# Odd attention: the second output projection begun inside the last block

## The chip, the cores and the metric

The kernel runs on one core of one Trainium2 chip. The metric is the time on the device, in microseconds, of one execution. Before the change it is 1584.4 us, the median of three runs (1583.5 to 1587.77).

## The reference

Two transformer layers work on `x` (512 tokens, width 1024) with a context of 256 tokens. Layer 0 is "even" (a gated MLP over chunks, and differential attention), layer 1 is "odd" (attention over a sliding window, with the context and a learned sink). Each layer ends with a SwiGLU network, and a last norm closes the block. The change lies in the odd layer and in the start of its SwiGLU:

```
def sink_attend(q, kvs, sink):                 # 16 heads, 4 KV heads, so 4 heads in a group
    ...                                        # scores of a block of 128 queries: window of up to 384 keys, masked, and 256 context keys
    p = softmax(concatenate(scores + [s_sink]))
    ...                                        # out = sum over the parts of p @ v

y = o.reshape(b, s_len, C_Q_WIDTH) @ w_out     # odd_mixer, 1024 x 1024
...
h = h + g1 * y
h = h + g2 * swiglu(modulate(h, norm2_g[l], sh2, sc2), ffn_w_in[l], ffn_w_out[l])
...
return rmsnorm(h, final_g)                     # modulate is rmsnorm(x, g) * (1 + scale) + shift
```

## The kernel before

Activations lie transposed in SBUF: 8 tiles of 128 features by 512 tokens. Every float32 product is made of three matmuls of rounded parts (`mm3`, lines L107, L108, L109): high weight by high input, high weight by low input, low weight by high input. So each input and each weight has a high and a low part. A weight block is loaded by SP's DMA queue into a "raw" tile (L78); ScalarE casts it to the high part (L81); the low part is a subtraction (L84), on GpSimd (POOL), or on VectorE where `dve_lo` says so (with 1, all of them). These tiles come from a ring of raw tiles and weight slots, `open_ring(width, raw, bufs)`; in the odd layer it has 3 raw tiles and 4 slots. `split` does the same for inputs: a cast on ScalarE (L123) and a subtraction on VectorE or POOL (L124).

`odd` projects keys, values and queries, and then computes attention. `attend(g, half)` handles one group of four heads for one half of the queries, in two blocks of 128 queries. For each head of a block `softmax` issues the scores (L1384, L1389, L1392), VectorE's maximum (L1395) and ScalarE's exponential (L1398). The exponentials are transposed on TensorE (L1421), copied out of PSUM by ScalarE or VectorE in turn (L1424), and multiplied with the values (L1432). Per group and half, a transposed row of reciprocals (L1439, L1443) scales the outcome (L1445).

All four groups run for the first half of the queries; `keep` splits their eight output tiles into `cat`. Then all four run for the second half. On TensorE the first half's output projection, `project(0, ...)`, is there to fill the gaps of the second half's attention: it takes the `fill` bank of PSUM (names `pf` in the profile). Then come, in the order of the program:

- `ffn_rstd`: the mean square of the first half's new residual (L157, L162), its inverse root on VectorE (L166 to L140), a diagonal of it (L177), and the product that spreads this over the partitions as a row (L187), into the same fill bank. This is "root's row" below.
- `catB`: eight `keep` of the second half, low parts in turn on VectorE and POOL.
- `ffn_open`, which starts the transfers of the SwiGLU's first weights (`ffn_in`, L817), their casts (L948) and subtractions (L952).
- `ffn_mod`: the modulation of the first half (L856 on VectorE, L857 on ScalarE, then L123 and L124).
- `project(1, ...)`: eight blocks of 8 x 3 matmuls of 256 columns, each followed by the residual (L778) and the square (L791, L795).

The SwiGLU's first products with the first half (the "direct" ones, of `ax` tiles) come next, then the second half's root, its row and its modulation, and the products with the second half (tiles `T` and others).

The order on each engine isn't that of the program. A scheduling layer moves instructions by a timeline of its own, within what the tile pools and banks allow; `issue_after` keeps what it encloses behind a given instruction. On each engine instructions then run in the order so fixed.

Of the kernel before, what the change touches and what calls it, by code (L numbers as in the profile page):

```python
# [15 lines left out]
D = 1024  # L16
KT = D // P
TX = 512
TC = 256
# [7 lines left out]
class Builder:  # L27
# [1275 lines left out]
    def odd(self):  # L1303
        tc, nc, a = self.tc, self.nc, self.a
        self.wp.release()
        self.open_wide()
        self.open_ring(512, 3, 4)
        X, C = [[[t[:, c] for t in A] for A in self.A] for c in (slice(0, TX), slice(TX, TA))]
        self.hcp.release()
        Rk = tc.alloc_tile_pool(name="kv1", bufs=1, side="right", reuse_waits="tile")  # L1310
# [13 lines left out]
        K = []  # L1324
# [31 lines left out]
        Qs = {}  # L1356

        def project_q(n):
            ps = self.fill()
# [5 lines left out]
        def softmax(g, i, rc):  # L1365
# [9 lines left out]
            for x in range(4):  # L1375
                pair, par = x // 2, x % 2
                if edge:
                    two = self.wide() if par == 0 else two
                    ps = two[:, par * TX:par * TX + TX]
                else:  # L1380
                    ps = self.wide()
                Q = Qs[2 * g + pair][par][:, i * P:(i + 1) * P]
                for p in range(2):
                    nc.tensor.matmul(ps[:, st:en], Q, K[g][p][:, b0 * P:b1 * P], start=p == 0, stop=p == 1,  # L1384
                                     skip_group_check=True)
                for b in range(b0, b1):
                    if b != i:
                        m0, c = (b - i + 1) * P, st + (b - b0) * P
                        nc.tensor.matmul(ps[:, c:c + P], identr, mask[:, m0:m0 + P], start=False, stop=True,  # L1389
                                         skip_group_check=True)  # L1390
                for p in range(2):
                    nc.tensor.matmul(ps[:, en:en + TC], Q, K[g][p][:, TX:], start=p == 0 and not edge, stop=p == 1,  # L1392
                                     skip_group_check=True)
                c = nm[:, x:x + 1]
                nc.vector.tensor_reduce(c, ps[:, st:en + TC], axis=AX, op=ALU.max, negate=True)  # L1395
                nc.vector.tensor_tensor(c, c, nsink[:, 4 * g + x:4 * g + x + 1], ALU.min)
                e = Rs.tile([P, 640], F32, name=self.uid("e"), tag="e1", bufs=7)
                nc.scalar.activation(e[:, :w + TC], ps[:, st:en + TC], AF.Exp, bias=c, accum_out=sums[:, x:x + 1])  # L1398
                es.append(e)
# [47 lines left out]
        raw = {}  # L1447

        def keep(half, n, eng):
            t = self.axp.tile([P, TA], F32R, name=self.uid("ax"), tag="ax", bufs=16)  # L1450
            t = t[:, :TC], t[:, TC:TX]
            self.split(*t, raw[half, n // 2][:, n % 2, :], eng)
            return t

        cat = []
# [7 lines left out]
            attend(g, 1)  # L1463
        sq = self.sumsq()

        def project(half, cat, bank):
            for m in range(KT):
                ps = bank(m)[:, :TC]
                self.dense(ps, self.blocks(a["odd_out"][m]), cat)
                self.residual(1, 2, m, half * TC, TC, ps)  # L1470
                self.square(sq, m, half * TC, TC, rest[half], (8, 7)[half])

        rest = [], []
        project(0, cat, lambda m: self.fill())
# [105 lines left out]
```

## Time and profile before

| | us |
|---|---|
| median of three runs | 1584.4 |
| the profiled execution | 1584.4 |
| its span | 1582.6 |
| TensorE busy (PE) | 1520.8 (96%) |
| VectorE busy (DVE) | 1080.4 (68%) |
| GpSimd busy (POOL) | 825.5 (52%) |
| ScalarE busy (ACT) | 725.9 (46%) |

The mean granted TensorE clock is 0.991. The odd layer's attention ends at about 1188 us, the projection of the second half follows up to about 1220, with the first SwiGLU products among its matmuls, and the SwiGLU of this layer takes the rest but for the last norm. TensorE's matmuls overlap, so the time from one start to the next, not an instruction's own duration, is its cost. In a row of the timeline the figure in square brackets is idle time of the engine just before, with what ended it. Buffer numbers are left out in the profile; in the changed program the attention's lines behind the scores have a number higher by one (L1421 is L1422, and so on).

### The profile page before, as it was taken

How to read it: one execution, taken by the hardware profiler on the slowest of the kernel's cores; microseconds unless marked ns; L12 is line 12 of the kernel's file. 1: busy time of each engine (PE TensorE's matmuls, PEld its weight loads, DVE VectorE, ACT ScalarE, POOL GpSimd, SP SyncE). 2: the span in 40 equal slices, each digit the busy share in tenths (PEclk: the TensorE clock that was granted, in tenths of full speed). 3: DMA queues.
4: the chain of work that ended last, by engine and by line, in shares of the span. 5: the costliest groups of instructions: out<-in, count | busy, mean ns of one | idle time of the engine just before them, and what ended most of it. 6: DMA issues, size and time to landing. Idle time of an engine off the chain costs nothing.

```text
span 1582.6 us, 25033 instructions
## 1 busy us (share of the span) xinstructions
PE 1520.8 (96%) x9575; PEld 1356.2 (86%) x9575; DVE 1080.4 (68%) x1951; ACT 725.9 (46%) x1477; POOL 825.5 (52%) x556
## 2 busy tenths in 40 slices
PE   6999988999999999999999989999999999999998
PEld 4676877889999999999999978777869989999997
DVE  3620788775697787888786495666568976666665
ACT  2422677553553333333333244556556544444444
POOL 0464211060347776777776415541304299898982
PEclk9999999999999999999999989999999999999999
DMA  9735100033123333454552012110225233333301
GB/s 329 309 128 202 44 8 1 1 133 134 67 74 120 113 109 118 139 160 143 165 167 67 27 52 80 61 34 8 68 76 197 65 112 106 99 105 107 98 21 54
DMA packets 53415, 162.26 MB, mean 103 GB/s; under 512 B 6192, under 2 KB 8624, under 8 KB 45616
## 3 DMA queue, kind: packets, MB, share of 16 engines
q1 hardware_dynamic: 46240, 135.37, 25.1%
q10 hardware_dynamic: 7056, 25.30, 4.9%
q8 instruction: 75, 1.23, 0.3%
q14 instruction: 44, 0.36, 0.1%
HBM read 158.55 MB, written 2.10 MB: 102 GB/s over the span
## 4 chain that ended last, share of the span: by engine, by line
PE 85%; DVE 9%; ACT 4%; issue 2%; DMA 0%; SPq 0%; POOL 0%; DVEq 0%; ACTq 0%; POOLq 0%
PE pw L107 11%; PE pw L108 11%; PE pw L109 11%; PE pb L108 8%; PE pb L109 8%; PE pb L107 8%; PE pf L107 4%; PE pf L108 4%; PE pf L109 4%; PE pb L1432 2%; PE pb L1421 2%; PE pf L363 2%; PE pw L1384 1%; PE pw L1392 1%; DVE t L883 1%
## 5 line engine op out<-in xcount | busy, mean ns | idle before, releaser
L84 POOL TENSOR_TENSOR w<-raw,w 128x512 fp32r<-128x512 f32 (+1 forms) x84 | 127.4, 1523 | 243.7 <-ACT w L81 221.7
L108 PE MATMUL pw<-ax,w 128*128 128x384 f32 (+2 forms) x732 | 234.6, 321 | 3.8 <-DVE ax L470 2.5
L107 PE MATMUL pw<-ax,w 128*128 128x384 f32 (+2 forms) x732 | 233.5, 323 | 4.1 <-DVE q L883 1.9
L109 PE MATMUL pw<-ax,w 128*128 128x384 f32 (+2 forms) x732 | 233.8, 320 | 0.1
L778 DVE SCALAR_TENSOR_TENSOR xT<-pb,mod,xT 128x512 f32<-128x512 f32 (+3 forms) x208 | 145.9, 707 | 125.8 <-PE pb L109 125.5
L883 POOL TENSOR_TENSOR w<-raw,w 128x512 fp32r<-128x512 f32 x110 | 169.0, 1551 | 19.7 <-ACT w L883 19.5
L883 POOL TENSOR_TENSOR w<-t,w 128x512 fp32r<-128x512 f32 x99 | 149.7, 1515 | 55.6 <-ACT w L883 55.6
L107 PE MATMUL pb<-hh,w 128*128 128x512 f32 x480 | 171.0, 356 | 1.2 <-DVE xT L778 1.2
L109 PE MATMUL pb<-hh,w 128*128 128x512 f32 x480 | 171.6, 357 | 0.3 <-DVE w L883 0.3
L108 PE MATMUL pb<-hh,w 128*128 128x512 f32 x480 | 171.2, 357 | 0.0
L108 PE MATMUL pw<-T,w 128*128 128x384 f32 (+1 forms) x508 | 157.1, 310 | 1.2 <-DVE T L124 1.2
L107 PE MATMUL pw<-T,w 128*128 128x384 f32 (+1 forms) x508 | 156.3, 310 | 1.1 <-DVE hs L883 1.1
L109 PE MATMUL pw<-T,w 128*128 128x384 f32 (+1 forms) x508 | 157.1, 310 | 0.0
L107 PEld LDWEIGHTS pw<-ax,w 128*128 128x128 f32 x732 | 138.9, 190 | 12.4 <-DVE q L883 2.6
L108 PEld LDWEIGHTS pw<-ax,w 128*128 128x128 f32 x732 | 139.3, 190 | 11.7 <-DVE ax L470 3.4
L107 PE MATMUL pf<-ax,w 128*128 128x256 f32 (+2 forms) x420 | 140.1, 333 | 8.5 <-DVE qf L256 5.7
L109 PEld LDWEIGHTS pw<-ax,w 128*128 128x128 f32 x732 | 139.5, 191 | 3.1 <-DVE w L952 0.4
L108 PE MATMUL pf<-ax,w 128*128 128x256 f32 (+2 forms) x420 | 138.9, 331 | 0.0
L109 PE MATMUL pf<-ax,w 128*128 128x256 f32 (+2 forms) x420 | 138.7, 330 | 0.0
L883 POOL TENSOR_TENSOR hh<-hs,hh 128x768 fp32r<-128x768 f32 (+1 forms) x42 | 80.2, 1910 | 90.0 <-ACT hh L883 67.6
L883 POOL TENSOR_TENSOR w<-rawo,w 128x512 fp32r<-128x512 f32 x59 | 103.7, 1758 | 28.7 <-ACT w L883 28.7
L232 DVE SCALAR_TENSOR_TENSOR junk<-ar,cb 128x1024 bf16<-128x1024 f32 x64 | 105.6, 1651 | 0.0
(376 smaller groups left out, 3937.1 us busy)
## 6 DMA issues: line engine op xcount, KB each, us to landing
raw<-ffn_in SPq DMA_DIRECT2D x44, 1024.0 KB, 5.2
ar<-ada SPq DMA_DIRECT2D x24, 1024.0 KB, 6.7
ar<-ada ACTq DMA_DIRECT2D x48, 512.0 KB, 3.6
rawo<-ffn_out SPq DMA_DIRECT2D x88, 256.0 KB, 3.0
raw<-odd_out SPq DMA_DIRECT2D x32, 256.0 KB, 2.7
raw<-qk SPq DMA_DIRECT2D x16, 256.0 KB, 8.2
raw<-uv SPq DMA_DIRECT2D x16, 256.0 KB, 2.7
raw<-even_out SPq DMA_DIRECT2D x8, 512.0 KB, 3.5
```

Of the source, the lines that this page charges most:

```text
L84: eng.tensor_tensor(lo, raw, hi.bitcast(F32), ALU.subtract)
L107: mm(out, s[0], m[0], start=start, stop=False, **kw)
L108: mm(out, s[0], m[1], start=False, stop=False, **kw)
L109: return mm(out, s[1], m[0], start=False, stop=stop, **kw)
L232: return self.nc.vector.scalar_tensor_tensor(junk, t, 1.0, self.cb[who], ALU.mult, ALU.mult, accum_out=self.acc[who][:, col:col + 1])
L363: nc.tensor.matmul(ps[32 * q:32 * q + 32, :w], cst[:, k, :], t[:, w * q:w * q + w], start=k == 0, stop=k == KT - 1, skip_group_check=True)
L778: ins = self.nc.vector.scalar_tensor_tensor(h, ps[:, r], self.modcol(l, j, m, who), h, ALU.mult, ALU.add)
L883: tail[key] = fn(*args, **kw)
L1384: nc.tensor.matmul(ps[:, st:en], Q, K[g][p][:, b0 * P:b1 * P], start=p == 0, stop=p == 1, skip_group_check=True)
L1392: nc.tensor.matmul(ps[:, en:en + TC], Q, K[g][p][:, TX:], start=p == 0 and not edge, stop=p == 1, skip_group_check=True)
L1421: last = nc.tensor.transpose(pt[:, x * P:(x + 1) * P], es[2 * (x % 2) + x // 2][:, kb * P:(kb + 1) * P], self.ident)
L1432: nc.tensor.matmul(po[64 * h:64 * h + 64, :], V[vb][:, 64 * g:64 * g + 64], t[:, h * TC:h * TC + TC], start=kb == 0, stop=kb == nb - 1, sk ...
```

## The change

Five things change in `odd`.

1. The ring gets 4 raw tiles and 5 slots instead of 3 and 4, for the whole layer.
2. `project(1)` begins early. For its blocks m = 0 and 1, the products with the first three groups' tiles (k = 0 to 5, 36 matmuls of 256 columns) go into the two halves of one fill bank, block m behind the last score matmul of head x = 1 (m = 0) or 2 (m = 1) in the last block of the last group. The products with the last group (k = 6, 7) and the residual follow when that group is done.
3. `catB` splits its first six tiles on VectorE alone (three of them were POOL's); the last two stay as they were.
4. `dve_lo` is set to 1 after the first early block instead of before `project(1)`.
5. Root's row is made behind all this, in a bank of `wide` instead of the fill bank; `ffn_mod` may issue only behind the split of the last group's first tile.

```diff
-        self.open_ring(512, 3, 4)
+        self.open_ring(512, 4, 5)
...
-                    nc.tensor.matmul(ps[:, en:en + TC], Q, K[g][p][:, TX:], start=p == 0 and not edge, stop=p == 1,
-                                     skip_group_check=True)
+                    last = nc.tensor.matmul(ps[:, en:en + TC], Q, K[g][p][:, TX:], start=p == 0 and not edge,
+                                            stop=p == 1, skip_group_check=True)
+                scored[g, i, x] = last
...
-            self.split(*t, raw[half, n // 2][:, n % 2, :], eng)
+            self.kept[n] = self.split(*t, raw[half, n // 2][:, n % 2, :], eng)
...
-        def project(half, cat, bank):
-            for m in range(KT):
+        def project(half, cat, bank, ready=()):
+            for m, ps, W in ready:
+                for k in (6, 7):
+                    self.mm3(ps, W[k], cat[k], False, k == 7)
+                self.residual(1, 2, m, half * TC, TC, ps)
+                self.square(sq, m, half * TC, TC, rest[half], (8, 7)[half])
+            for m in range(len(ready), KT):
...
-        self.ffn_rstd(sq, rest[0], TX // 2)
-        catB = [keep(1, n, nc.gpsimd if n % 2 else nc.vector) for n in range(8)]
+        dg = self.rstd_diag([(sq[:, :TC], TC)], 1.0 / D, self.fill, None, None, rest[0])[0]
+        catB = [keep(1, n, nc.vector) for n in range(6)]
+        both, ready, mark = self.fill(), [], None
+        for m in range(2):
+            W = self.blocks(a["odd_out"][m])
+            ps = both[:, m * TC:(m + 1) * TC]
+            with tc.issue_after(scored[(3, *((3, 1), (3, 2))[m])].ins):
+                for k in range(6):
+                    with tc.issue_after(mark.ins) if mark else ExitStack():
+                        ins = self.mm3(ps, W[k], catB[k], m == k == 0, False)
+            mark = ins
+            ready.append((m, ps, W))
+            if m == 0:
+                self.dve_lo = 1
+        catB += [keep(1, n, nc.gpsimd if n % 2 else nc.vector) for n in range(6, 8)]
+        self.r = self.spread(dg, self.wide)
         Rs.release()
         Rk.release()
         self.ffn_open(1)
-        self.ffn_mod(1, 0)
-        self.dve_lo = 1
-        project(1, catB, lambda m: self.bank())
+        with tc.issue_after(self.kept[6].ins):
+            self.ffn_mod(1, 0)
+        project(1, catB, lambda m: self.bank(), ready)
```

On TensorE, in the last block of the last group, these instructions stood between the last scores (`pw_11235` with `qb_10320`) and the first product with the last head's transposed weights (`pt_11264`). `e_11252` is the exponential of those last scores.

```order
L1392 MATMUL pw_11235<-kh_9187,qb_10320 128x256
L1392 MATMUL pw_11235<-kl_9188,qb_10320 128x256
L1421 MATMUL pb_11259<-ident_100,e_11243 128x128
L1421 MATMUL pb_11259<-ident_100,e_11233 128x128
L1421 MATMUL pb_11266<-ident_100,e_11243 128x128
L1421 MATMUL pb_11266<-ident_100,e_11233 128x128
L1421 MATMUL pb_11259<-ident_100,e_11252 128x128
L1421 MATMUL pb_11266<-ident_100,e_11252 128x128
L1432 MATMUL pb_11258<-pt_11264,v_2_9364 64x256 x2
```

Now 29 of the early matmuls stand ahead of those scores. Behind the scores, after two transposes and one more early matmul, TensorE has this up to the first transpose of `e_11252`; `pf_11653` is the fill bank, and L187 is root's row.

```order
L107 MATMUL pf_11653<-ax_11647,w_11689 128x256
L1433 MATMUL pb_11166<-pt_11204,v_5_9370 64x256 x2
L1422 MATMUL pb_11266<-ident_100,e_11224 128x128
L1422 MATMUL pb_11266<-ident_100,e_11243 128x128
L1422 MATMUL pb_11266<-ident_100,e_11233 128x128
L108 MATMUL pf_11653<-ax_11647,w_11689 128x256
L109 MATMUL pf_11653<-ax_11647,w_11689 128x256
L107 MATMUL pf_11653<-ax_11650,w_11689 128x256
L108 MATMUL pf_11653<-ax_11650,w_11689 128x256
L109 MATMUL pf_11653<-ax_11650,w_11689 128x256
L187 MATMUL pw_11716<-q_11632,ones 128x256
L1422 MATMUL pb_11259<-ident_100,e_11252 128x128
```

Seven early matmuls, root's row, one more transpose (L1422) and the two products L1433 have come in between.

On VectorE, at the end of the attention, the last group's scaling (L1445) stood behind the eight L856 of the modulation. What is shown begins with the last two of these.

```order
L856 SCALAR_TENSOR_TENSOR hh_11671<-xT_636_3306,mod_69,pf_11635 128x256
L856 SCALAR_TENSOR_TENSOR hh_11670<-xT_636_3306,mod_69,pf_11635 128x256
L1445 TENSOR_TENSOR o_11113<-o_11113,pb_11296 128x512
L84 TENSOR_TENSOR w_11797<-raw_11795,w_11797 128x512
L124 TENSOR_TENSOR ax_11655<-o_11113,ax_11655 128x256
```

Now the scaling and the first split come first, then the L856, whose last two are shown with what follows:

```order
L856 SCALAR_TENSOR_TENSOR hh_11728<-xT_636_3306,mod_69,pw_11716 128x256
L856 SCALAR_TENSOR_TENSOR hh_11727<-xT_636_3306,mod_69,pw_11716 128x256
L84 TENSOR_TENSOR w_11840<-raw_11838,w_11840 128x512
L124 TENSOR_TENSOR ax_11737<-hm_11734,ax_11737 128x256
L778 SCALAR_TENSOR_TENSOR xT_633_3300<-pf_11653,mod_69,xT_633_3300 128x256
L84 TENSOR_TENSOR w_11874<-raw_11872,w_11874 128x512
L778 SCALAR_TENSOR_TENSOR xT_634_3302<-pb_11793,mod_69,xT_634_3302 128x256
```

The L856 have moved behind L1446 (L1445 before) and the split of the last group's first tile.

On ScalarE, the casts of the first `ffn_in` weights (L948) stood early in the second projection, between casts of its weights (`w_11802`, `w_11836`):

```order
L81 CAST w_11802<-raw_11800 128x512
L948 CAST w_12038<-raw_11666 128x512
L948 CAST w_12041<-raw_11666 128x512
L948 CAST w_12044<-raw_11666 128x512
L948 CAST w_12047<-raw_11666 128x512
L81 CAST w_11836<-raw_11834 128x512
```

Now they stand behind the casts of all its weights and behind the squares (L791) of all residuals but the last:

```order
L81 CAST w_11996<-raw_11994 128x512
L791 ACTIVATE q_11907<-xT_635_3304 128x256
L791 ACTIVATE q_11946<-xT_635_3304 128x256
L791 ACTIVATE q_11985<-xT_636_3306 128x256
L948 CAST w_12037<-raw_11723 128x512
L948 CAST w_12040<-raw_11723 128x512
```

The first of them waits until the projection's seventh block (m = 6) has released the slot that the tile takes; POOL's subtractions L952 follow them.

More of the change, by code (lines that the diff above doesn't have):

```diff
@@ L1355, in odd @@
         Rs = tc.alloc_tile_pool(name="att1", bufs=1, side="right", reuse_waits="tile")
-        Qs = {}
+        Qs, scored = {}, {}
         def project_q(n):
@@ L1445, in attend @@
             nc.vector.tensor_tensor(o, o, ps, ALU.mult)
-        raw = {}
+        raw, self.kept = {}, {}
         def keep(half, n, eng):
```

## The prediction

> **What bounds the kernel now.** I first read the page: the share of each engine and the chain of work that ended last.
>
> ```profile
> PE 1520.8 (96%) x9575; PEld 1356.2 (86%) x9575; DVE 1080.4 (68%) x1951; ACT 725.9 (46%) x1477; POOL 825.5 (52%) x556
> PE 85%; DVE 9%; ACT 4%; issue 2%; DMA 0%; SPq 0%; POOL 0%; DVEq 0%; ACTq 0%; POOLq 0%
> ```
>
> TensorE is busy for 1520.8 of 1582.6 us and makes up 85% of the chain. The change neither adds a product nor takes one away: the 36 matmuls that it starts early are among the 192 that followed the attention. So it can only win or lose time in which TensorE stands still, or runs at a lower clock. I looked for that time with the busy table in 10 us stretches around the end of the attention (columns: length, PE, PEld, DVE, ACT, POOL, granted clock, DMA share, GB/s).
>
> ```profile
> 1180.00:1190.00 10.00, 7.90 (x49) 4.76 (x48) 5.36 (x15) 3.91 (x10) 0.61 (x1) 0.83 0.56 211
> 1190.00:1200.00 10.00, 8.36 (x63) 7.53 (x63) 8.96 (x13) 10.00 (x26) 7.09 (x7) 1.00 0.39 131
> 1270.00:1280.00 10.00, 8.10 (x58) 7.26 (x57) 9.90 (x14) 4.74 (x10) 9.93 (x7) 1.00 0.48 158
> ```
>
> TensorE loses 2.1 us in 1180-1190, where the clock also falls to 0.83, and 1.6 us in 1190-1200. In 1270-1280 it loses 1.9 us, and there VectorE is the full engine (9.90). The list of TensorE's waits in 1150-1290 names five of the losses (us in total, times, longest); its timeline shows the others, in brackets, and what follows them.
>
> ```profile
> PE pw L107 <- DVE q L883: 1.9, 1, 1.9
> PE pb L109 <- DVE w L84: 1.6, 1, 1.6
> PE pw L107 <- DVE hs L883: 1.1, 1, 1.1
> PE pf L187 <- DVE sa L1400: 1.1, 1, 1.1
> PE pb L109 <- DVE w L883: 0.3, 1, 0.3
> ```
>
> ```profile
> 1165.62 0.65 PE L1432 MATMUL pb<-pt,v 128*64 128x256 f32 x4
> 1166.20 0.66 PE L1421 MATMUL pb<-ident,e 128*128 128x128 f32 x4
> ...
> 1182.07 0.44 PE L1421 MATMUL pb<-ident,e 128*128 128x128 f32 x2 [1.48 <-ACT e L1398]
> 1183.13 0.65 PE L1432 MATMUL pb<-pt,v 128*64 128x256 f32 x4 [0.62 <-ACT pt L1424]
> 1183.72 0.74 PE L1421 MATMUL pb<-ident,e 128*128 128x128 f32 x4
> 1184.39 1.12 PE L1432 MATMUL pb<-pt,v 128*64 128x256 f32 x4
> 1185.44 1.11 PE L1421 MATMUL pb<-ident,e 128*128 128x128 f32 x4
> 1186.48 1.60 PE L1432 MATMUL pb<-pt,v 128*64 128x256 f32 x8
> 1188.01 0.66 PE L1443 MATMUL pb<-ident,pt 128*128 128x128 f32 x4
> 1188.63 0.28 PE L108 MATMUL pb<-ax,w 128*128 128x256 f32 x1
> ...
> 1189.93 0.28 PE L107 MATMUL pb<-ax,w 128*128 128x256 f32 x1
> ```
>
> The last block of the last group of heads has no other matmuls left to issue. TensorE stands 1.48 us while the exponential of the last scores runs, then 0.62 us for a copy of the transposed weights. Right after, the same instructions take nearly twice as long: four L1432 take 1.05 us from start to start (1184.39 to 1185.44) against 0.58 at 1165.62, and four L1421 are busy for 1.11 us against 0.66. Two stretches of 2 us show why; the seventh column is the granted clock.
>
> ```profile
> 1184.00:1186.00 2.00, 2.00 (x11) 0.99 (x10) 0.00 (x0) 0.58 (x1) 0.07 (x1) 0.54 1.02 426
> 1186.00:1188.00 2.00, 2.00 (x11) 0.74 (x9) 1.41 (x4) 0.00 (x0) 0.00 (x0) 0.61 0.98 410
> ```
>
> **Part by part.** The rows are those of the profiled execution, which took 1584.4 us (span 1582.6, 1.8 around it). That is also the median of the three runs, so the sum needs no shift.
>
> *The fill in the last block.* A projection matmul on 256 columns starts every 0.118 us (1188.63 to 1189.93, 11 steps). The 36 early ones are 4.3 us, moved from behind the attention into its last block, in themselves worth nothing. 29 of them stand ahead of the last scores and only delay these. The other 7 (0.8 us) stand between the last scores and the first transpose that needs the exponential, along with L1433 x2 (0.3), one more transpose (0.15) and root's row (0.5) that did not stand there. That makes 1.8 us for a wait of 1.48 us. The exponential comes a little later itself, because ScalarE now has a cast of 0.6 us of an output weight ahead of it; I allow 0.2 us. 1.8 covers 1.7, barely: **-1.5** (bounds 0 and -1.5). The 0.62 us wait on the copy has the same work around it as before, and stays.
>
> *The clock.* Against full speed the slow steps lose 0.47 (L1432 x4), 0.45 (L1421 x4) and 1.53 - 1.16 = 0.37 us (L1432 x8), together **-1.3** if the clock stays up (bounds 0 and -1.4). It fell after 2.1 us of standing in 2.5 us. The waits of 1.6 and 1.9 us in the list lie in 1190-1200 and 1270-1280, whose clock is 1.00. With 0.6 to 0.7 us left here I expect no drop.
>
> [...]
>
> *Root's row and the modulation.* The row (L187) leaves this place:
>
> ```profile
> 1163.99 0.67 PE L187 MATMUL pf<-q,ones 128*128 128x256 f32 x2 [1.09 <-DVE sa L1400]
> 1164.50 0.38 PE L1421 MATMUL pb<-ident,e 128*128 128x128 f32 x2
> 1163.55 0.69 ACT L1398 ACTIVATE e<-pw,sa 128x512 f32<-128x512 f32 x1 [2.31 <-DVE sa L1396]
> ```
>
> The transposes behind it can't start before their exponential ends at 1164.24, so its 0.51 us gives back only 0.26 here, and costs 0.51 in the last block: **+0.3** (bounds 0 and +0.5). VectorE's eight L856 (3.2 us), which stood ahead of the last block's own output (L1445), now stand behind it and the first subtraction of catB; nobody on the path waits for them until the first ffn_in product. Three subtractions of catB pass from POOL to VectorE, some 0.4 us each (the L795 below has their shape), while VectorE is half idle (5.36 in 1180-1190). SP's first transfers of ffn_in now queue behind an output weight whose slot comes free in the last block, some 4 us later than before; they land in 5.2 us and are first read over 20 us on, so that costs nothing.
>
> ```profile
> raw<-ffn_in SPq DMA_DIRECT2D x44, 1024.0 KB, 5.2
> ```
>
> *The projection after the attention.* These rows carry it (VectorE and POOL):
>
> ```profile
> 1197.29 1.66 DVE L84 TENSOR_TENSOR w<-raw,w 128x512 fp32r<-128x512 f32 x1
> 1198.88 1.78 DVE L952 TENSOR_TENSOR w<-raw,w 128x512 fp32r<-128x512 f32 x1
> 1207.15 0.68 DVE L84 TENSOR_TENSOR w<-raw,w 128x512 fp32r<-128x512 f32 x1
> 1207.75 0.41 DVE L795 TENSOR_TENSOR sq<-sq,q 128x256 f32<-128x256 f32 x1
> 1209.87 0.48 DVE L778 SCALAR_TENSOR_TENSOR xT<-pb,mod,xT 128x256 f32<-128x256 f32 x1
> 1197.14 9.80 POOL L952 TENSOR_TENSOR w<-raw,w 128x512 fp32r<-128x512 f32 x6
> ```
>
> A weight's subtraction on VectorE takes 0.68 us alone and 1.66 to 1.78 us while POOL subtracts too, and the late one stops TensorE for the 1.6 us of the list. In the changed order POOL's L952 come only after the sixth block of the projection, and the weights of the first 46 matmuls behind the attention have been subtracted within it. But VectorE's queue gets tight. From its L1446 to the residual of the seventh block stand 9 L84 (6.1 us), 8 L856 (3.2), 7 L778 (3.4), 5 L124 (2.1), 4 L795 (1.6) and L1446 (0.7): 17.1 us, less some 0.08 us overlap for each of 34 (1207.15 + 0.68 against 1207.75), so 14.4. POOL's five L124 will slow one or two of them by 1 us: about 16 us, against 134 matmuls or 15.8 us of TensorE. I expect half the wait to come back in small pieces: **-0.8** (bounds 0 and -1.6; the first rival has it above zero).
>
> *VectorE's lead into the FFN.* 45 matmuls now lie between the second root's row and the first product with the second half, 30 before; so VectorE's modulation starts 15 x 0.118 = 1.8 us earlier against TensorE.
>
> ```profile
> 1229.88 0.87 DVE L856 SCALAR_TENSOR_TENSOR hm<-xT,mod,pb 128x256 f32<-128x256 f32 x2 [1.72 <-PE pb L187]
> 1252.65 0.41 DVE L989 TENSOR_TENSOR hs<-hs,pw 128x256 f32<-128x256 f32 x1
> ```
>
> From 1229.88 VectorE works without a gap to 1252.65, and TensorE then waits for it 0.3 + 1.1 + 1.9 = 3.3 us over the next 25 us (the list's L883). What starts 1.8 us earlier should end so, unless ScalarE or POOL step in: **-1.2** (bounds 0 and -1.8).
>
> *The larger ring* takes effect at the start of the layer:
>
> ```profile
> 955.11 0.62 ACT L81 CAST w<-raw 128x512 fp32r<-128x512 f32 x1 [3.07 <-issue]
> 957.42 0.39 PE L108 MATMUL pw<-ax,w 128*128 128x256 f32 x1 [0.72 <-DVE ax L205]
> 984.73 0.47 PE L107 MATMUL pf<-ax,w 128*128 128x512 f32 x1 [2.62 <-DVE qf L256]
> ```
>
> ScalarE stood 3.07 us on a cast whose slot was taken, behind which the normalised inputs queue that TensorE waits 0.72 us for. A fifth slot frees the cast: **-0.7**. POOL's order shifts as well, by one or two subtractions of 1.3 us ahead of the rotated keys on which the 2.62 us wait rests: bounds -0.7 and +1.0.
>
> Sum: -1.5 - 1.3 + 0.3 - 0.8 - 1.2 - 0.7 = -5.2; 1584.4 - 5.2 = **1579.2 us**. All terms at their good ends: -1.5 - 1.4 - 1.6 - 1.8 - 0.7 = -7.0, 1577.4. A measurement of this kernel tells about 0.3% (4.75 us) from no change, so the forecast lies close to that limit.
>
> **The rivals.**
>
> *VectorE falls behind (slower).* If POOL's five L124 each slow a neighbour by 1 us and nothing overlaps, VectorE needs up to 17.1 + 4 = 21.1 us for TensorE's 15.8. The point that decides is whether its residual of the seventh block is done when TensorE gets there. Then TensorE waits 5.3 us instead of 1.6 (+3.7). The first ffn_in weights follow on: their L948 casts now stand behind the square of that residual (0.4), then 0.55 for the cast and 1.63 for POOL (9.80 / 6), while TensorE needs them 27 matmuls (3.2 us) after the seventh block; 1.1 us more. The clock drops there (+1.3), and the lead is lost: -1.5 - 1.3 + 0.3 - 0.7 + 3.7 + 1.1 + 1.3 = +2.9, **1587.3**. For it speaks that VectorE is 8.96 full in 1190-1200; against, that the 1.7 us subtractions came beside POOL's ten us of L952, which are gone from there. Chance 0.15.
>
> *The clock drop stays* or moves to another pause: -5.2 + 1.3, **1580.5**. Chance 0.13. For: the drops' exact cause isn't in the trace. Against: it follows the pauses directly.
>
> *The fill only moves the wait (the change doesn't do what it says).* 29 of 36 matmuls delay the last scores; if the exponential comes 1.5 us later behind the new cast, TensorE still stands 1.3 us and the clock drops: -5.2 + 1.3 + 1.3, **1581.8**. Chance 0.12.
>
> **How the numbers follow.** The forecast with its terms between the bounds has 0.60. It is centred at 1579.2 and about 1.8 us wide to each side, so that it is beyond 0.3% in somewhat over half: with what the rivals add, 0.40 faster. The two rivals at 1580.5 and 1581.8 and the rest of the forecast make no change, with most of the slow rival: 0.49. Slower by over 0.3% needs the slow rival and something beyond its price: 0.11. The range goes from the good ends less what the lowest run lies below the median (1584.4 - 1583.5 = 0.9), 1576.5, to the slow rival's 1587.3.
>
> **What would show it.** Right: the wait of L1422 for the exponential is gone or below 0.3 us, the clock is 1.00 in the whole last block, no wait for a weight's subtraction exceeds 0.8 us in the projection, the first ffn_in products wait for nothing, and the waits for VectorE before 1275 fall to about 2 us. Wrong: a clock below 0.9 anywhere from the last scores to the FFN, waits for L84 or L952 beyond 1.6 us, a later first query projection, or a loss in the FFN itself, where the order of every queue shifts and I have worked out nothing.

## The result: 0.2% slower, not 0.3% faster

The changed kernel takes 1587.99 us in the median of 18 runs (1586.64 to 1592.77), the kernel before 1584.94 us beside it (18 runs, 1582.26 to 1590.19). The ratio is 1.0022, with a 95% interval of 1.0015 to 1.0029: slower by 3.1 us, inside the 0.3% that the prediction called no change. The forecast was 1579.2 and the range ended at 1587.3, so both missed, and the sign is the other one.

The profiled execution of the changed kernel took 1588.2 us (span 1586.2) against 1584.4 (1582.6). On the page TensorE looks the same as before:

```profile
PE 1521.2 (96%) x9575; PEld 1357.0 (86%) x9575; DVE 1079.5 (68%) x1952; ACT 726.7 (46%) x1477; POOL 823.3 (52%) x555
PE 85%; DVE 9%; ACT 3%; issue 1%; DMA 0%; POOL 0%; DVEq 0%; SPq 0%; ACTq 0%; POOLq 0%
```

**Where to count from.** Up to the odd layer both programs are the same, row for row. Yet root's row of the layer's first norm starts at 935.15 us after and at 932.86 before: 2.29 us of the difference arose before the first changed instruction. In all profiles of this study that point lies between 930.9 and 935.7 us. So everything below is counted from it. "Start" is what a kernel has lost (+) against before when the scores of the second head in the last block of the last group are issued, ahead of which no early matmul stands; "tail" is what it loses or gains from there to the hundredth product with the second half in the SwiGLU; "end" is the sum at the program's last matmul.

Counted so, the changed kernel has a start of **+6.1**, a tail of **-4.6** and an end of **+1.5** us. The tail is what the prediction was about. The loss lies 150 us ahead of it.

**The end of the attention and behind it.** The table of 10 us stretches shows no half clock any more (1.00 in both rows, where 1180-1190 had 0.83), and the stretch 1190-1200 with the end of the last block is fuller (columns: length, PE, PEld, DVE, ACT, POOL, clock, DMA share, GB/s):

```profile
1180.00:1190.00 10.00, 9.87 (x77) 7.65 (x76) 5.86 (x15) 5.88 (x15) 0.00 (x0) 1.00 0.02 3
1190.00:1200.00 10.00, 9.18 (x69) 6.37 (x68) 4.04 (x9) 3.40 (x9) 0.62 (x1) 1.00 0.64 251
```

The timeline of the last block shows the early matmuls and root's row between the transposes. The exponential's transposes (1193.64) no longer wait; the copy still costs 0.62 us.

```profile
1192.73 0.28 PE L109 MATMUL pf<-ax,w 128*128 128x256 f32 x1
...
1193.21 0.59 PE L187 MATMUL pw<-q,ones 128*128 128x256 f32 x2
1193.64 0.38 PE L1422 MATMUL pb<-ident,e 128*128 128x128 f32 x2
1194.64 0.65 PE L1433 MATMUL pb<-pt,v 128*64 128x256 f32 x4 [0.62 <-ACT pt L1425]
1195.23 0.66 PE L1422 MATMUL pb<-ident,e 128*128 128x128 f32 x4
1195.81 0.65 PE L1433 MATMUL pb<-pt,v 128*64 128x256 f32 x4
```

Four L1422 take 0.58 us from start to start (1195.23 to 1195.81): full speed. TensorE's waits from 940 to 1300 name no weight's subtraction any more. At their head stands something else:

```profile
PE pf L107 <- DVE qf L256: 10.2, 4, 5.8
PE pb L1422 <- ACT e L1399: 2.5, 4, 1.5
PE pw L107 <- DVE q L883: 1.9, 1, 1.9
...
PE pw L107 <- DVE hs L883: 1.0, 1, 1.0
...
PE pb L187 <- DVE q L177: 0.4, 1, 0.4
```

The transposes' waits for exponentials (L1422) come to 2.5 us in four, as they did before (L1421). The last block's 1.48 us is gone, but another of the same length has come some 20 us earlier, where root's row and its own wait of 1.09 us stood:

```profile
1172.81 0.44 PE L1422 MATMUL pb<-ident,e 128*128 128x128 f32 x2 [1.48 <-ACT e L1399]
```

So that place gives back 1.09 + 0.51 - 1.48 = 0.1 us.

**The start of the layer.** The waits of the query projections on the rotated queries (qf L256) were 5.7 us in four before:

```profile
PE pf L107 <- DVE qf L256: 5.7, 4, 2.6
```

The busy table shows the clock in three stretches there. First before:

```profile
980.00:990.00 10.00, 7.38 (x26) 5.65 (x25) 4.52 (x7) 3.80 (x6) 6.05 (x5) 0.83 0.25 79
990.00:1000.00 10.00, 9.00 (x46) 7.45 (x45) 6.50 (x9) 5.63 (x10) 6.05 (x5) 1.00 0.17 55
1010.00:1020.00 10.00, 9.51 (x51) 7.80 (x51) 7.96 (x16) 5.11 (x11) 6.94 (x7) 1.00 0.24 73
```

Then after, where it is low in all three, and TensorE has less to do in each:

```profile
980.00:990.00 10.00, 4.51 (x20) 3.39 (x19) 7.45 (x10) 5.04 (x8) 7.19 (x5) 0.83 0.16 53
990.00:1000.00 10.00, 8.73 (x33) 7.06 (x34) 3.94 (x8) 2.50 (x4) 4.89 (x5) 0.83 0.17 52
1010.00:1020.00 10.00, 7.80 (x37) 6.43 (x36) 7.19 (x11) 4.72 (x11) 5.13 (x4) 0.87 0.17 54
```

How the order made this can be read from the timeline of all engines. First the kernel before, from the first value product to the first rotated query:

```profile
955.83 0.34 PE L107 MATMUL pb<-w,ax 128*128 128x256 f32 x1
969.00 1.31 POOL L258 TENSOR_TENSOR kf<-kf,sh 128x512 f32<-128x512 f32 x1
971.20 4.07 DVE L283 TENSOR_TENSOR kl<-kf,kh 64x768 fp32r<-64x768 f32 x4 [7.11 <-ACT kh L280]
976.94 1.29 POOL L258 TENSOR_TENSOR kf<-kf,sh 128x512 f32<-128x512 f32 x1 [0.51 <-DVE kf L256]
979.13 4.07 DVE L283 TENSOR_TENSOR kl<-kf,kh 64x768 fp32r<-64x768 f32 x4 [1.62 <-ACT kh L280]
983.90 0.69 DVE L256 TENSOR_TENSOR qf<-pf,cos 128x512 f32<-128x512 f32 x1
```

Then the changed kernel (take 2.29 us off each start to compare):

```profile
946.91 0.99 PE L107 MATMUL pb<-w,ax 128*128 128x256 f32 x2
961.25 1.34 ACT L81 CAST w<-raw 128x512 fp32r<-128x512 f32 x2 [2.30 <-issue]
968.50 2.54 POOL L84 TENSOR_TENSOR w<-raw,w 128x512 fp32r<-128x512 f32 x2
972.24 1.28 POOL L258 TENSOR_TENSOR kf<-kf,sh 128x512 f32<-128x512 f32 x1
974.42 2.14 DVE L283 TENSOR_TENSOR kl<-kf,kh 64x768 fp32r<-64x768 f32 x2 [7.14 <-ACT kh L280]
976.78 2.72 DVE L283 TENSOR_TENSOR kl<-kf,kh 64x768 fp32r<-64x768 f32 x2 [0.22 <-ACT kh L280]
980.18 1.30 POOL L84 TENSOR_TENSOR w<-raw,w 128x512 fp32r<-128x512 f32 x1 [2.47 <-ACT w L81]
981.44 1.29 POOL L258 TENSOR_TENSOR kf<-kf,sh 128x512 f32<-128x512 f32 x1
986.56 2.89 DVE L283 TENSOR_TENSOR kl<-kf,kh 64x768 fp32r<-64x768 f32 x2
989.46 0.69 DVE L256 TENSOR_TENSOR qf<-pf,cos 128x512 f32<-128x512 f32 x1
990.30 0.77 PE L107 MATMUL pf<-ax,w 128*128 128x512 f32 x1 [5.79 <-DVE qf L256]
1017.27 0.78 PE L107 MATMUL pf<-ax,w 128*128 128x512 f32 x1 [2.20 <-DVE qf L256]
```

The fifth slot lets a weight of the values be cast early, and the value products (`pb<-w,ax`) begin at 946.91 among the keys', 11.2 us earlier. The next weight's cast follows behind all normalised inputs (961.25). So POOL does subtractions of weights (968.50, 980.18) just when the keys' rotation needs it: the first rotated key is 0.95 us later, the second 2.2. VectorE's subtractions of the keys (L283), one block of 4.07 us before, now take 5.1 us from 974.42 to 979.50, in two pieces beside POOL's, and 5.8 us the second time with a shuffle between. The first rotated query comes 3.27 us late, and with it the second query projection. A later one (1017.27) waits 2.20 instead of 0.86, and half a clock behind it (0.50 from 1017.32 to 1020.73) costs 1.6 more. That makes 3.3 - 0.1 + 1.3 + 1.6 = 6.1 us. The first 3.3 can be followed back to the moved order in these rows. The other 2.9 can't with the same right: ring_v below, which holds the value products back, has the same later wait (2.23 us).

The profiled pair thus differs by 1.5 us from the common point on, the medians by 3.1. The mean clocks fit the larger figure (0.988 over the 18 runs after, 0.989 to 0.990 over the runs before in each set), but in which place the other executions lose it one profile each can't show.

### The profile page after: what moved, and what is told of

The parts are those of the page before. It is cut to its first block, busy times and chain, and to the rows that moved or that the text cites. A ratio compares the mean times of both kernels' runs of the same rounds, so it can differ in the third digit from the quotient of the medians.

```text
span 1586.2 us, 25027 instructions
## 1 busy us (share of the span) xinstructions
PE 1521.2 (96%) x9575; PEld 1357.0 (86%) x9575; DVE 1079.5 (68%) x1952; ACT 726.7 (46%) x1477; POOL 823.3 (52%) x555
## 4 chain that ended last, share of the span: by engine, by line
PE 85%; DVE 9%; ACT 3%; issue 1%; DMA 0%; POOL 0%; DVEq 0%; SPq 0%; ACTq 0%; POOLq 0%
PE pw L107 11%; PE pw L108 11%; PE pw L109 11%; PE pb L108 8%; PE pb L107 8%; PE pb L109 8%; PE pf L107 4%; PE pf L108 4%; PE pf L109 4%; PE pb L1433 2%; PE pb L1422 2%; PE pf L363 2%; PE pw L1384 1%; PE pw L1392 1%; PE pw L546 1%
## 5 line engine op out<-in xcount | busy, mean ns | idle before, releaser
L84 POOL TENSOR_TENSOR w<-raw,w 128x512 fp32r<-128x512 f32 (+1 forms) x86 | 131.1, 1532 | 249.4 <-ACT w L81 224.3
L108 PE MATMUL pw<-ax,w 128*128 128x384 f32 (+2 forms) x732 | 233.8, 320 | 3.5 <-DVE ax L205 2.1
L778 DVE SCALAR_TENSOR_TENSOR xT<-pb,mod,xT 128x512 f32<-128x512 f32 (+3 forms) x206 | 144.9, 709 | 128.5 <-PE pb L109 128.2
L883 POOL TENSOR_TENSOR w<-raw,w 128x512 fp32r<-128x512 f32 x110 | 169.4, 1556 | 20.3 <-ACT w L883 20.2
L883 POOL TENSOR_TENSOR w<-t,w 128x512 fp32r<-128x512 f32 x99 | 148.9, 1507 | 55.5 <-ACT w L883 55.5
L108 PE MATMUL pb<-hh,w 128*128 128x512 f32 x480 | 171.3, 357 | 0.0
L108 PE MATMUL pw<-T,w 128*128 128x384 f32 (+1 forms) x508 | 157.3, 310 | 1.2 <-DVE T L124 1.2
L107 PE MATMUL pf<-ax,w 128*128 128x256 f32 (+2 forms) x436 | 145.5, 334 | 13.0 <-DVE qf L256 10.2
L108 PEld LDWEIGHTS pw<-ax,w 128*128 128x128 f32 x732 | 139.1, 190 | 10.7 <-DVE ax L205 3.1
L108 PE MATMUL pf<-ax,w 128*128 128x256 f32 (+2 forms) x436 | 143.8, 330 | 0.0
L109 PE MATMUL pf<-ax,w 128*128 128x256 f32 (+2 forms) x436 | 143.7, 330 | 0.0
L883 POOL TENSOR_TENSOR hh<-hs,hh 128x768 fp32r<-128x768 f32 (+1 forms) x42 | 78.6, 1871 | 91.3 <-ACT hh L883 68.8
L883 POOL TENSOR_TENSOR w<-rawo,w 128x512 fp32r<-128x512 f32 x59 | 103.5, 1755 | 30.5 <-ACT w L883 30.5
```

The lines of the kernel that those rows point to most:

```text
L84: eng.tensor_tensor(lo, raw, hi.bitcast(F32), ALU.subtract)
L107: mm(out, s[0], m[0], start=start, stop=False, **kw)
L108: mm(out, s[0], m[1], start=False, stop=False, **kw)
L109: return mm(out, s[1], m[0], start=False, stop=stop, **kw)
L778: ins = self.nc.vector.scalar_tensor_tensor(h, ps[:, r], self.modcol(l, j, m, who), h, ALU.mult, ALU.add)
L883: tail[key] = fn(*args, **kw)
```

## The experiments

In the first set: **A** says that the larger ring alone loses the time at the start; the other readings leave the loss to chance in one execution, to the fill and the move, or to where the tiles lie in memory. All kernels, counted as above (us; the row "changed kernel" is for comparison):

| kernel | ratio (95%) | start | tail | end |
|---|---|---|---|---|
| changed kernel | 1.0022 (1.0015-1.0029) | +6.1 | -4.6 | +1.5 |
| ring_only | 1.0029 (1.0018-1.0040) | +6.8 | -1.9 | +5.0 |
| old_ring | 1.0001 (0.9992-1.0009) | -1.0 | +1.5 | +0.5 |
| late_ring | 0.9972 (0.9961-0.9984) | -1.3 | -2.9 | -4.2 |
| fill_only | 0.9994 (0.9985-1.0004) | -1.5 | -1.4 | -1.3 |
| late_ring_b | 0.9989 (0.9980-0.9999) | -2.1 | -2.7 | -3.2 |
| pool_order | 0.9991 (0.9983-1.0000) | +2.6 | -4.0 | -1.4 |
| v_late | 0.9964 (0.9951-0.9978) | -2.4 | -4.6 | -7.0 |
| v_late_2 | 0.9971 (0.9959-0.9983) | -2.2 | -4.5 | -6.7 |
| both_back | 0.9992 (0.9983-1.0000) | +3.3 | -4.1 | -0.8 |
| ring_v | 0.9984 (0.9973-0.9995) | +1.3 | -0.7 | +0.6 |
| ring_v_move | 0.9992 (0.9978-1.0006) | -1.7 | -1.8 | -2.0 |
| ring_v_fill | 0.9990 (0.9981-1.0000) | -2.2 | -1.7 | -2.4 |

The ratios rest on 5 (v_late), 6 (v_late_2) or 8 (late_ring) to 18 runs of a kernel, and are not quite the quotients of the medians given below. Start, tail and end are of one profile each, and for ring_only, v_late and v_late_2 the profiled run is the fastest of the kernel.

How much chance is in a start can be seen in kernels of the same order. On all engines, before, old_ring, late_ring, fill_only and late_ring_b run the same order for 180 us behind root's row; their starts go from 0 to -2.1, and the kernel before, from which all are counted, is the slowest of them. The four kernels with the value products held and the whole ring (v_late, v_late_2, ring_v_move, ring_v_fill; both_back has further holds) have -1.7 to -2.4, and ring_v, in the same order as they, +1.3. The two with the larger ring and nothing held have +6.1 and +6.8, clear of both groups.

### ring_only: the ring alone

```diff
 # in the kernel before
-        self.open_ring(512, 3, 4)
+        self.open_ring(512, 4, 5)
```

> The kernel before with the larger ring (4 raw tiles, 5 slots) and nothing else of the change. Theory A, the ring's new order at the start of the layer costs the time: counted from root's row of the normalisation, the changed kernel's profile loses 6.1 us up to the sixth query projection, and the ring alone brings the same order there; so about 6 us over before, 1591 +- 2, with waits on qf of 8 to 11 us in all (5.7 before). Rival B, the loss is chance of one execution (the changed profile was already 2.3 us late before the first changed instruction, and the clock's half windows move freely): within 2 us of before. Rival C, the loss comes from the parts behind the attention: no more than 1 us here.

1589.41 us against 1585.33. The start loses 6.8 us, with the same wait for the queries as in the changed kernel, to the tenth; the wait of root's row (L187) is untouched, as it should be.

```profile
PE pf L107 <- DVE qf L256: 10.2, 4, 5.8
PE pf L187 <- DVE sa L1400: 1.1, 1, 1.1
```

A holds: the loss is the ring's, and chance and the parts behind the attention fall as its causes. Not foreseen: the ring alone already takes 1.9 us off the tail; the weights behind the attention are no longer late (the 1.6 us wait for w L84 is gone).

### old_ring: everything but the ring

```diff
 # in the changed kernel
-        self.open_ring(512, 4, 5)
+        self.open_ring(512, 3, 4)
```

> The changed kernel with the old ring (3 raw tiles, 4 slots) throughout. Up to the last groups its order is that of the kernel before. Theory A: the start loses nothing, and most of the 4.6 us that the changed profile regains behind the attention stays: 1580 to 1582. Rival D, the early matmuls need the fifth slot, without which their weights come late: 1584 to 1587, with waits of TensorE on w in the last block or just behind it. Rival B: as the changed kernel, 1587 to 1588.

1586.61 against 1585.33, as rival D had it. The start's loss is gone, and the attention's end gains as in the changed kernel (-2.2). Then the second projection gives it back; its weights and the SwiGLU's first inputs are late, and half a clock follows at 1237.4 (0.51 for 3.4 us):

```profile
PE pw L107 <- ACT T L123: 1.5, 1, 1.5
PE pb L109 <- DVE w L84: 1.3, 2, 0.9
PE pw L107 <- DVE hh L856: 1.1, 1, 1.1
PE pw L108 <- DVE T L124: 1.1, 1, 1.1
```

So the fill in the last block does without the fifth slot, but what follows it needs the slot. The loss at the start and the gain in the tail hang on the same line of code, unless the slot comes later.

### late_ring: the fifth slot only from the second projection on

```diff
 # in the changed kernel: 3 and 4 at the layer's start; a fourth raw tile and a
 # fifth slot under tags of their own, in rotation from project(1) on
-        self.open_ring(512, 4, 5)
+        self.open_ring(512, 3, 4)
...
+        self.more = 1
         for m in range(2):
-            W = self.blocks(a["odd_out"][m])
+            with tc.issue_after(expd[2, 2, 0].ins):
+                W = self.blocks(a["odd_out"][m])
```

> The changed kernel with the old ring up to the first half's projection; the fourth raw tile and the fifth slot join it only for the second half's output weights, and the casts of the first four of these are held behind an exponential of the third group. The ring's pool in SBUF is as large as in the changed kernel; the order at the start is that of before, the order from the early matmuls on that of the changed kernel. Theory A (order): start 0, tail -4.6, so 1580.3 +- 1.5. Rival E, not the order but the larger pool's place in SBUF makes the start wait for other tiles: the start loses 6 us as in the changed kernel, 1586 to 1589. Rival B: 1583 to 1587.

1581.98 against 1585.33, faster than both kernels, and 0.2 us above what A allowed. The ring takes as much memory as in the changed kernel and the start's loss is gone, so it isn't the place where other tiles then lie that costs. 1.7 us of the tail's 4.6 are missing. Two waits for the first SwiGLU weights are new, 1.1 us together (lines are 9 higher here); the last projection block still holds the slot that these weights take.

```profile
PE pw L116 <- ACT w L957: 0.7, 1, 0.7
PE pw L118 <- POOL w L961: 0.4, 1, 0.4
```

### fill_only: late_ring without the move

```diff
 # in late_ring
         dg = self.rstd_diag([(sq[:, :TC], TC)], 1.0 / D, self.fill, None, None, rest[0])[0]
+        self.r = self.spread(dg, self.wide)
...
-        self.r = self.spread(dg, self.wide)
...
-        with tc.issue_after(self.kept[6].ins):
-            self.ffn_mod(1, 0)
+        self.ffn_mod(1, 0)
```

> As the kernel with the late ring, but root's row is spread where it was made, ahead of the last block, and the modulation isn't held behind the last group. So of the change there remain the early matmuls, the splits on VectorE and the earlier dve_lo. Theory A with the prediction's terms: the wait for the exponential (1.5) and the half clock (1.3) are gone, and little else: 1581.5 to 1582.5. Rival F, where the row and the modulation stand makes no difference: 1580.3, as the late ring. Rival G, the L856 ahead of the last group's scaling cost more than a microsecond now that the last block is tighter: 1583 or more.

1583.57, above A's bounds and F's time. The attention's end gains (net -2.4 there), but 1.5 us of tail are lost against late_ring, and behind the table's tail half a clock at 1274.0 (0.51 for 3.4 us) costs 1.5 more. New beside late_ring are waits for a residual (xT L787, 1.0 us) and a weight (w L93, 0.7); that the L856 cause them, as G would have it, isn't shown. The ratio's interval lies above late_ring's, so the move is worth something beside the fill.

### late_ring_b: another place for the extra slot

```diff
 # in late_ring
-            if self.more % 5 == 2:
+            if self.more % 5 == 3:
```

> The late ring with the extra slot taken by the second of the early weights instead of the first. So the first cast of ffn_in weights waits for the sixth block of the projection (m = 5) to leave its slot, not for the last (m = 7). In the late ring's profile TensorE waits 0.7 us for that cast and 0.4 for POOL's subtraction behind it, and from the attention's end to the second root's row it is 1.7 us slower than the changed kernel. If these waits are what it lacks: 1.0 to 1.7 us below the late ring, 1580 to 1581. If something else is: as the late ring, 1582.

1582.64; it was to be faster than late_ring and isn't. The waits for L957 and L961 have gone (0.2 is left), and two others stand in their place:

```profile
PE pb L118 <- DVE w L93: 0.9, 1, 0.9
PE pb L116 <- ACT w L90: 0.7, 1, 0.7
```

So those two waits were not by themselves what late_ring lacks.

### pool_order, v_late and both_back: which part of the moved order costs

With the ring at 4 and 5 from the start, pool_order holds POOL's subtractions so that its order is that of before (A1: they are what delays the rotation), and v_late holds the value products behind the keys (A2: the early value products are the root of it). both_back does both.

```diff
 # pool_order, in the changed kernel (the same for the queries' weights)
-            W = self.blocks(a["v1"][kq], step=256)
+            W = self.blocks(a["v1"][kq], step=256, hold=(None, self.turns[t0][0] if kq else None))
 # v_late, in the changed kernel; late is the fifth context product of the second key block
-                    self.mm3(acc[tb], A, W[i], k == 0 and tb % 2 == 0, k == KT - 1)
+                    with tc.issue_after(late.ins):
+                        self.mm3(acc[tb], A, W[i], k == 0 and tb % 2 == 0, k == KT - 1)
```

> The changed kernel with one thing put back at the start of the layer: POOL's order. Its weight subtractions are held so that POOL runs the rotation of keys and queries (L257, L258) in the same place among them as before the change; in the changed kernel one more weight subtraction stands ahead of each. The value projection's matmuls stay early, among the keys'. Theory A1, POOL's order makes the rotated keys and with them the query projections late: the start's 6 us are gone, 1580.5 to 1582.5, waits on qf 5 to 6 us in all (10.2 in the changed kernel). Theory A2, the early value matmuls push the keys back: 1586 to 1588, waits on qf as in the changed kernel.

> The changed kernel with the other thing put back: the value projection's matmuls are held where they were before the change, behind the second key block's fifth product with the context. POOL keeps weight subtractions ahead of the rotations, in part as in the changed kernel (two instead of one between the second key block's L256 and its L258). Theory A1 (POOL's order): at least half of the 6 us stay, 1584 to 1587. Theory A2 (the early value matmuls): the start loses nothing, 1580.5 to 1582.

> The changed kernel with both put back: POOL's order and the place of the value matmuls, with the larger ring. Theory A: start 0, tail -4.6, so 1580.3 +- 1.5. If the larger ring costs in another way (its casts, its transfers), 1583 or more.

pool_order takes the start's loss away up to the sixth query projection (-0.5 there), but the holds change the order of the queries behind it, and the first half's attention loses 3 us: 1583.66, between A1's bounds and A2's. Nor is its start quite that of before. The second query projection still waits 4.56 us, and VectorE's L283 take 5.06 and 6.04 us, 0.99 and 1.97 more than the 4.07 before: three of the eight run beside a subtraction of POOL and take 1.9 us each, where the median before is 0.955.

v_late is the fastest kernel of the study: 1578.51 against 1585.34. I had expected at least half the start's loss to stay in it, and all of it went. POOL's order came back by itself with the value products: no two subtractions stand ahead of the rotated key any more, and VectorE's L283 are whole.

```profile
969.40 1.29 POOL L258 TENSOR_TENSOR kf<-kf,sh 128x512 f32<-128x512 f32 x1
971.59 4.07 DVE L283 TENSOR_TENSOR kl<-kf,kh 64x768 fp32r<-64x768 f32 x4 [6.04 <-ACT kh L280]
979.04 4.06 DVE L283 TENSOR_TENSOR kl<-kf,kh 64x768 fp32r<-64x768 f32 x4 [1.67 <-ACT kh L280]
984.63 0.47 PE L107 MATMUL pf<-ax,w 128*128 128x512 f32 x1 [3.15 <-DVE qf L256]
```

So A2 holds: without the value products' early start the loss at the start is gone, in v_late and again in v_late_2. That it reaches the queries by way of POOL's subtractions, ahead of the rotated keys (A1) and beside L283, is read from the timelines; these kernels can't take the two apart. both_back (1584.25, where 1580.3 was expected) has pool_order's loss in the attention again (+3.3), so the holds themselves cost.

### ring_v, ring_v_move, ring_v_fill, v_late_2: what each part is worth with the start mended

```diff
 # ring_v: the kernel before, with ring 4 and 5 and the value products held
 # ring_v_move: ring_v and the row and modulation moved (no early matmuls)
 # ring_v_fill: v_late without the move
 # v_late_2: v_late again, on another chip
```

> The kernel before with the larger ring and the value projection's matmuls held where they stood: no early matmuls, root's row and modulation as before. Theory H, the larger ring does two things, a loss at the start through the value matmuls and a gain behind the attention, where the projection's weights come in time: the start at 0 to -2.4 (as in the profile with the values held), behind the attention -1.9 (as in the ring alone), together 1581 to 1583. Rival I, the gain behind the attention needs the early matmuls: 1583 to 1585.

> As before plus the larger ring, the values held, and root's row and the modulation moved behind the attention; no early matmuls, and the splits and dve_lo as before. The prediction's terms: the wait for the exponential (1.5) stays or shrinks by the row's 0.5, the clock may drop, and VectorE's lead grows: 0.5 to 1.5 below the ring with the values held. Rival J, the modulation behind the attention delays the last VectorE work that the projection needs: the same or 1 us above it.

> The changed kernel with the values held, but root's row spread where it was made and the modulation not held back: the early matmuls without the move. The prediction's terms: the wait for the exponential and the half clock there are gone, so up to 2.8 below the ring with the values held, and 1 to 2 above the full change with the values held: 1579.5 to 1581. Rival F, the move makes no difference: as the full change, 1578.5.

> The changed kernel with the values held, once more, for its place beside the other three on one chip and for a second profile of the clock at the first query projections. In its first profile the 3.2 us wait there had no half clock behind it, in the profile before 2.6 us had one. If that is chance, it may have one now, and the start is then 0 to -1 instead of -2.4; the times stay at 1577.5 to 1580.

1582.56, 1581.80, 1583.11 and 1580.34, against 1584.25. v_late's gain comes again (0.9971), though the time is 0.3 us above its bounds, and its start is -2.2, not the 0 to -1 that a half clock at the first queries was to bring. ring_v lies within H's time but has neither part as H had it (start +1.3, tail -0.7); ring_v_fill was to be 1579.5 to 1581 and is 2 us above. The ring with the values held gains 0.1 to 0.2% alone, with the move or with the fill, and of these ring_v_move's interval holds 1 and ring_v_fill's ends there. Only both together reach 0.3%; the intervals of ring_v and v_late_2 overlap, so the step between these two is likely rather than shown. In the profiles each of the three has something in the tail that v_late or v_late_2 lacks: ring_v has a clock of 0.50 from 1183.6 to 1190.4, where v_late has 1.00 from 1180 to 1210; ring_v_move still waits 3.5 us in three for exponentials behind 1100, v_late_2 2.0 in two; ring_v_fill waits for a residual (xT L778, 1.0 us) and a weight (w L84, 0.7), v_late for neither. ring_v's start of +1.3 comes from a longer wait at the fifth query projection, 0.86 us before and absent in v_late:

```profile
1011.27 0.50 PE L107 MATMUL pf<-ax,w 128*128 128x512 f32 x1 [2.23 <-DVE qf L256]
```

Its order there is v_late's, and so is ring_v_move's; these two wait 5.4 and 5.6 us in all for rotated queries, ring_v 7.6. Why the wait comes in ring_v stays open.

## Why the prediction was wrong, step by step

- *The fill in the last block (-1.5), the clock (-1.3), root's row (+0.3)*: right in sum. At the attention's end the changed kernel is 8.1 us behind, of which 6.1 are the start's and 36 x 0.118 = 4.2 are moved matmuls: -2.2. By the prediction's terms, with the row's full 0.51 us in the block, it was -2.3. The wait for the exponential is gone from the last block, the one for the copy is 0.62 as said, and the clock stayed up. old_ring, late_ring, late_ring_b and v_late have the same -2.2. Where the row left, 0.1 us came back instead of 0.26.
- *The projection behind the attention (-0.8) and VectorE's lead (-1.2)*: the sum was near, -2.4 against -2.0, the parts weren't. The wait for the weight went wholly (-1.6). VectorE's earlier start did little: of 0.3, 1.1 and 1.9 us only the 0.3 went, and 0.4 came anew at L187. Some 0.9 us more went inside TensorE's busy time, where no wait shows it. In ring_only the larger ring alone does 1.9 us of this step, which I had credited to the move of POOL's L952.
- *The larger ring (-0.7, bounds -0.7 to +1.0)*: **this term failed.** It measured +6.1, and +6.8 by itself in ring_only. The prediction saw POOL's subtractions ahead of the rotated keys and priced them at one or two of 1.3 us, softened. It left out that the value products move in among the keys', that VectorE's L283 then run in part beside POOL's work, that a later query can be late as well, and that the clock would read 0.50 there for 10.2 us (986.60 to 993.42 and 1017.32 to 1020.73) instead of 3.4. The -0.7 itself didn't come either: the wait of 0.72 us went, but another for the normalised inputs (L108, 942.83), behind one more early cast (ScalarE's L81 at 939.35), grew from 0.57 to 1.76 us, and the first query projection starts 0.1 us later than before.
- *The rivals*: VectorE falling behind in the tail did not happen, nor did the clock drop stay, nor did the wait only move. What happened was in the list of signs ("a later first query projection"; it is the second that is late) and in no rival. The slow rival's sum has a slip: five neighbours slowed by 1 us each make 5 us, not 4, and so 1588.3 for the end of the range. The 1587.99 would then have lain inside by luck, with a loss that the rival doesn't have. -5.2 with +6.1 in place of -0.7 would have given 1586.0; the medians have 1588.0.
- *The SwiGLU*: nothing is lost there; the +1.5 us at its hundredth product is +1.5 at the end.

## What to carry to other kernels

A resource that is widened for one stage (a slot, a raw tile) is widened for every stage that shares it, and where a scheduler fills freed slots the order changes at the first place that can use one. So follow the order from the first changed instruction, not from the edit that you care about, and give the widened resource the term with the widest bounds. When a change has a good part and a bad part on the same line, keep the good one by pinning the order where the bad one arises: the value products held behind the keys turned +0.2% into -0.3%.

## What the runs showed of the hardware

**Pauses of like length had half clock behind them in one place and full clock in another.** In before the granted clock reads 0.50 for 3.4 us soon after the wait of 2.62 us at the second query projection, and again after the 1.48 and 0.62 us in the last block:

```profile
986.18:989.60 3.42, 3.42 (x10) 2.64 (x9) 0.00 (x0) 0.63 (x2) 1.91 (x2) 0.50 0.26 89
1184.15:1187.57 3.42, 3.42 (x17) 1.54 (x16) 0.98 (x2) 0.58 (x1) 0.00 (x0) 0.50 1.02 426
```

In after it reads 0.50 for 6.8 us, beginning within the wait of 5.79, and for 3.4 us after the one of 2.20:

```profile
986.60:993.42 6.82, 3.12 (x7) 2.49 (x8) 4.40 (x5) 1.45 (x3) 5.21 (x3) 0.50 0.13 38
1017.32:1020.73 3.41, 3.41 (x8) 2.74 (x9) 2.86 (x7) 1.52 (x4) 1.81 (x2) 0.50 0.01 5
```

In the first of these four stretches the matmuls of 512 columns start every 0.43 us, before and behind it every 0.23. The eight that start in it lose 1.6 us; the second stretch lost 1.3. The same 1.9 us wait for L883 (L892 in fill_only) shows both outcomes. In fill_only half clock follows it:

```profile
1270.60:1274.00 3.40, 1.50 (x10) 1.06 (x9) 3.30 (x5) 1.97 (x4) 3.40 (x3) 1.00 0.43 117
1274.00:1277.40 3.40, 3.40 (x13) 2.91 (x13) 3.40 (x5) 0.93 (x2) 3.29 (x4) 0.51 0.31 70
```

In v_late the clock stays, and in before, where the same wait is 1.90 us, 1270-1280 has 1.00:

```profile
1262.65:1266.06 3.41, 1.59 (x7) 0.94 (x5) 3.41 (x5) 1.96 (x4) 3.41 (x3) 1.00 0.30 82
1266.06:1269.48 3.42, 3.33 (x22) 3.06 (x23) 3.31 (x6) 0.00 (x0) 3.42 (x4) 1.00 0.31 81
```

Nor does the 3.15 us wait at v_late's second query projection have half clock behind it (1.00 from 980 to 1000), where 2.62 us in before did. The 24 matmuls behind it take 5.64 us in v_late (984.63 to 990.27) and 7.17 in before (984.73 to 991.90). Less the 0.53 us by which the wait is longer, that is 1.0 us of v_late's start of -2.4. What decides whether the clock falls after a pause, these rows don't show.

Such stretches also lie elsewhere in another execution of the same instructions, as rival B of ring_only has it. Ahead of the first changed one, after has one behind a wait of 2.26 us for xT (L778), where before waits 1.20 and has full clock (after first, then before):

```profile
467.77:471.18 3.41, 3.41 (x13) 3.41 (x14) 2.72 (x4) 1.39 (x3) 3.41 (x3) 0.50 0.30 77
460.00:480.00 20.00, 18.80 (x108) 17.09 (x107) 15.41 (x19) 7.54 (x14) 20.00 (x13) 1.00 0.43 144
```

**The identical first 930 us differed between executions**, by 2.29 us between before (932.86) and after (935.15) and by up to 4.8 us over all profiles (930.9 to 935.7); the mean clock of one kernel's runs differed by up to 0.006 (before: 0.987 to 0.993). So differences of 2 us between two profiles mean something only from a common point on.
